# A pair of seven-product sets for the indexer's two column groups, and one operation for the low parts of a turned block

## The chip, the cores and the metric

The kernel runs on one core of a Trainium2 chip, as one launch. The metric is the device time of the launch in microseconds, the median of several runs. The core's engines work from queues of their own and wait for each other only where one needs what another made: TensorE (PE, with PEld for its weight loads), VectorE (DVE), ScalarE (ACT), GpSimd (POOL) and SyncE (SP), whose queue issues nearly all DMAs.

## The reference: what is computed

Two layers over 256 tokens of 2048 features, everything in float32. Each layer is a mixer and an MLP, each behind an RMS norm and added to the residual:

```
for i in range(DEPTH):                      # DEPTH = 2
    h = rms_norm(x, norm_mix[i])
    x = x + (stick_breaking_mixer if i % 2 == 0 else dsa_mixer)(h, ...)
    h = rms_norm(x, norm_mlp[i])
    x = x + square(relu(h @ w_up[i])) @ w_down[i]      # 2048 -> 8192 -> 2048
```

The change is in the second mixer, `dsa_mixer`:

```
q, k, v, qi, ki, wi = split(h @ w_in, [2048, 512, 512, 1024, 64, 16])
q = rms_norm(q, q_gain);  k = rms_norm(k, k_gain)      # per head of 128
score = sum over 16 heads of wi * relu(qi . ki)        # the indexer, heads of 64
sel   = the 64 best keys of each token, chunk-causal
p     = softmax(q . k[sel] + bias);  out = (p @ v[sel]) @ w_out
```

The indexer's queries `qi` are 1024 columns of that projection: two groups of 512.

## The kernel before, in words

**Splitting.** A float32 product is made of three products of rounded operands: activation and weight are each split into a high part and the rest. The activations lie transposed, as `xT` (features on the partitions, 16 tiles of 128, high and low part). A weight arrives block by block: an *item* is one block of 256 rows by 512 columns, held as 128 x 1024. SP loads it to `wraw` (L2006), ACT writes its high part `wh` (L2023), DVE the rest, `wl` (L2024). PE then does 12 matmuls of 512 columns (L628; L619 where an item is first in its section): 8 with `wh` against high and low activation, then 4 with `wl`. There are four buffers each for `wh` and `wl`, so the split of an item can start once the matmuls of the fourth one before it are through. A column group of 512 over the 2048 features is 8 items.

**Seven products.** In the MLPs, the output projection and the first mixer, two column groups of one matrix are mostly taken as a *pair*: of the 8 row blocks four go in two sets, `a` and `b`, and in each set a 2 x 2 block product is done with seven products (Winograd's form of Strassen's), not eight. A product has 6 matmuls; its weight is a sum of blocks (the rooms X, Y, Z: three DVE additions, L973, L976, L985, and one addition in an accumulating DMA on POOL's queue), its activation a sum S of blocks of `xT` (one whole addition and four quarter additions on DVE, L1079 and L1049 to L1052, then a split of the sum on ACT, L1060, and DVE, L1064). Half of the products are read back through seeds (copies of an accumulator, L1011 to L1028). The names `s1a` to `s7b` are the products of the two sets, `G0` to `G3` and `H0` to `H3` the items that stay plain.

**The second mixer.** `mixer_b` runs, before the change: 16 plain items for `qi` (two groups side by side), two short items for `ki` and `wi`, 8 items for `k`, then `q0 q1 q2 v q3` of 8 items each, and last the output projection, which is done in a pair already. Behind an item other work is hung (`post`): `k_done` (norm of k: two scalings L1783, 8 squares with sums on ACT L1789, small steps for the root, a product L1795, two transposes, a DMA round trip), `score_step` (L1739: 8 matmuls a call, then ACT and DVE), the choice of the 64 best, `logits_step` (L1851), `turn_step`, `o_step` (L1901 to L1903).

**Borders.** Where a section ends, its four column blocks c0 to c3 of the residual become the next section's `xT`: DVE adds the accumulators to the residual `xs` (L937, in the MLP L1335) and transposes in 32 x 32 blocks (L492); SP writes to DRAM in four DMAs (`tu<-jx`, L499) and reads back turned (`jx<-tu`, L504); ACT writes the high part with the gain in 4 operations (L524), DVE the low part in 8 (L529). ACT takes the squares for the norm (L908, L566).

**Order.** The program is unrolled. A planner (`Plan`) gives each piece of this work a slot behind an item, from costs and due times (`LAT`, `AHEAD`, `CALM`), and every engine then works its queue strictly in the order of that program. The main loop loads `far` items ahead and splits a few items ahead of PE. A scheduler may move PE's matmuls a little.

## Time and profile before

| | us |
|---|---|
| median of three runs (1988.82 to 1989.66) | 1989.25 |
| span of the profiled execution | 1986.8 |
| of it PE busy | 1980.4 |
| DVE busy | 1785.0 |
| ACT busy | 1301.7 |
| POOL busy | 91.7 |
| second mixer on PE, first matmul to the next section's first | 1028.39 to 1327.30 |

The span lies 2.45 us below the median of the runs. A row of the timeline has the start, the time until the last instruction of the row is done, the engine, the line, the operation, output and input, and how many instructions the row holds; behind it, in brackets, how long the engine stood idle before it, and what ended that. Engines are pipelined: the next operation can start some 0.1 us before the printed end of the one ahead. In the table of windows, the columns are busy time and instructions (x) of each engine, then the granted PE clock, the DMA share and the rate.

### The profile page before, as it was taken

To read this page: it belongs to the slowest core of one execution; us is meant where nothing else is said; L and a number is where in the kernel's file an instruction comes from. 1 tells how busy PE (TensorE), PEld (TensorE's weight loads), DVE (VectorE), ACT (ScalarE), POOL (GpSimd) and SP (SyncE) were. 2 spreads that over 40 slices of the span, in tenths; PEclk is the share of its full clock that TensorE was granted. 3 is DMA by queue.
4 is the path that set the end of the run, shared out by engine and by line. 5 is a ranking of instruction groups with operands and counts; after the bars stand their busy time and mean duration, and the time that the engine had idled before them with its cause. 6 is when DMAs were issued, how large, how long until landed. Compare 5 with 4: busy or idle time off the path is not lost.

```text
span 1986.8 us, 25525 instructions
## 1 busy us (share of the span) xinstructions
PE 1980.4 (100%) x8834; PEld 1635.3 (82%) x8834; DVE 1785.0 (90%) x1973; ACT 1301.7 (66%) x1573; POOL 91.7 (5%) x135
## 2 busy tenths in 40 slices
PE   9999999999999999999999999999999999999999
PEld 7888888888888888888888788788888888888887
DVE  6879869899999999989995898889998998998996
ACT  6567666667676676766764566666767676776664
POOL 0000100000000000020000000000000000000000
PEclk9999999999999999999999999999999999999999
DMA  9776766889788977889887698578887888788784
GB/s 350 215 238 189 218 211 181 275 289 292 244 259 257 278 235 239 288 277 295 247 291 235 190 264 255 153 264 281 290 265 244 254 269 271 224 286 276 256 244 146
DMA packets 233441, 498.44 MB, mean 251 GB/s; under 512 B 88608, under 2 KB 121440, under 8 KB 233312
## 3 DMA queue, kind: packets, MB, share of 16 engines
q1 hardware_dynamic: 216048, 455.81, 68.8%
q0 software_dynamic: 9216, 33.56, 9.4%
q10 hardware_dynamic: 8048, 7.45, 1.1%
q8 instruction: 69, 1.13, 0.2%
q14 instruction: 60, 0.49, 0.1%
HBM read 459.46 MB, written 37.22 MB: 250 GB/s over the span
## 4 chain that ended last, share of the span: by engine, by line
PE 99%; DVE 0%; DMA 0%; issue 0%; ACT 0%; SPq 0%; DVEq 0%
PE acc L1169 39%; PE acc L1151 26%; PE acc L628 17%; PE acc L732 5%; PE aux L1151 4%; PE aux L751 2%; PE acc L751 1%; PE acc L619 1%; PE aux L1851 0%; PE acc L1494 0%; PE aux L1554 0%; PE acc L1739 0%; PE aux L1169 0%; PE acc L1704 0%; PE aux L1556 0%; PE acc L1496 0%
## 5 line engine op out<-in xcount | busy, mean ns | idle before, releaser
L2024 DVE TENSOR_TENSOR wl<-wraw,wh 128x1024 fp32r<-128x1024 f32 (+1 forms) x670 | 805.5, 1217 | 134.6 <-ACT wh L2023 121.9
L2023 ACT ACTIVATE wh<-wraw 128x1024 fp32r<-128x1024 f32 (+1 forms) x670 | 700.0, 1053 | 317.8 <-PE acc L1169 110.7
L1169 PE MATMUL acc<-wh,xT 128*128 128x512 f32 x1152 | 284.6, 389 | 0.0
L1169 PEld LDWEIGHTS acc<-wh,xT 128*128 128x128 f32 x1152 | 216.2, 188 | 45.2 <-ACT wh L2023 0.3
L1169 PE MATMUL acc<-wh,half 128*128 128x512 f32 x1004 | 248.2, 389 | 0.0
L1169 PEld LDWEIGHTS acc<-wh,half 128*128 128x128 f32 x1004 | 188.5, 188 | 39.1
L1151 PE MATMUL acc<-wh,half 128*128 128x512 f32 x720 | 192.4, 389 | 0.0
L628 PE MATMUL acc<-wh,xT 128*128 128x512 f32 x736 | 185.5, 392 | 0.0
L628 PEld LDWEIGHTS acc<-wh,xT 128*128 128x128 f32 x736 | 137.6, 188 | 30.0 <-issue 1.7
L1151 PEld LDWEIGHTS acc<-wh,half 128*128 128x128 f32 x720 | 135.2, 188 | 28.1
L1169 PE MATMUL acc<-wl,xT 128*128 128x512 f32 x576 | 154.0, 389 | 0.0
L1169 PE MATMUL acc<-wl,half 128*128 128x512 f32 x502 | 134.4, 389 | 0.0
L1169 PEld LDWEIGHTS acc<-wl,xT 128*128 128x128 f32 x576 | 108.1, 188 | 22.5
L1151 PE MATMUL acc<-wl,half 128*128 128x512 f32 x360 | 110.8, 389 | 0.0
L1169 PEld LDWEIGHTS acc<-wl,half 128*128 128x128 f32 x502 | 94.2, 188 | 19.5
L628 PE MATMUL acc<-wl,xT 128*128 128x512 f32 x368 | 99.2, 391 | 0.0
L2023 ACT ACTIVATE wh<-Zb 128x1024 fp32r<-128x1024 f32 x60 | 63.5, 1058 | 41.5 <-PE acc L1169 14.4
L1151 PE MATMUL acc<-wh,xT 128*128 128x512 f32 x336 | 89.8, 389 | 0.0
L628 PEld LDWEIGHTS acc<-wl,xT 128*128 128x128 f32 x368 | 68.9, 188 | 15.0 <-DVE wl L2024 0.3
L732 PE MATMUL acc<-wh,xT 128*128 128x512 f32 x320 | 79.7, 391 | 0.0
L1151 PEld LDWEIGHTS acc<-wl,half 128*128 128x128 f32 x360 | 67.6, 188 | 14.0
L2024 DVE TENSOR_TENSOR wl<-Za,wh 128x1024 fp32r<-128x1024 f32 x60 | 73.4, 1223 | 0.7 <-ACT wh L2023 0.6
(404 smaller groups left out, 3087.2 us busy)
## 6 DMA issues: line engine op xcount, KB each, us to landing
wraw<-in_w_up_dram SPq DMA_DIRECT2D x228, 512.0 KB, 5.4
wraw<-in_w_down_dram SPq DMA_DIRECT2D x224, 512.0 KB, 5.1
wraw<-in_w_in_a_dram SPq DMA_DIRECT2D x88, 512.0 KB, 4.9
wraw<-in_w_in_b_dram SPq DMA_DIRECT2D x64, 512.0 KB, 4.8
jx<-tu SPq DMA_DIRECT2D x44, 512.0 KB, 5.8
tu<-y SPq DMA_DIRECT2D x128, 128.0 KB, 3.6
wraw<-in_w_out_a_dram SPq DMA_DIRECT2D x30, 512.0 KB, 3.6
wraw<-in_w_out_b_dram SPq DMA_DIRECT2D x30, 512.0 KB, 4.4
```

Of the source, the lines that this page charges most:

```text
L619: pin(pe.matmul(accs[key][t], L[:, j, part, t * P:(t + 1) * P], wx[:, j, :], start=(j == 0 and n == 0), stop=False))
L628: (keep if alone else pin)(pe.matmul(acc[t], L[:, KB * q + j, part, t * P:(t + 1) * P], wx[:, j, :], start=a and q == 0, stop=z and q == Q ...
L732: keep(pe.matmul(acc[:, t, :], L[:, KB * qs[i] + j, part, t * P:(t + 1) * P], wx[:, j, :], start=a and i == 0, stop=z and i == end - (last ...
L751: keep(pe.matmul(p, lhs(part, j), wx[:, j, :], start=to is None and a and n == sets[0], stop=to is None and z and n == sets[-1]))
L1151: keep(pe.matmul(o, lhs(part, j), wx[:, j, :], start=a and opens, stop=z, skip_group_check=True))
L1169: keep(pe.matmul(acc[:, t, :], L[:, KB * q + j, part, t * P:(t + 1) * P], wx[:, j, :], start=a and i == 0 and not self.sets, stop=z, skip_ ...
L2023: order(act.activation(wh[:, a], raw[:, a], AF.Copy))
L2024: order(dve.tensor_sub(wl[:, a], raw[:, a], wh[:, a].bitcast(F32)))
```

## The change

- `mixer_b` begins with `k` and `qi` together, in the order `ORDER_QI`. The two column groups of `qi` are a pair with two sets: 14 products of 6 matmuls and 8 plain items of 12 take the place of 16 plain items. The 8 items of `k` stand singly among the products, so `k` is complete, and `k_done` runs, behind `k7`, ahead of `s7a`; the short items for `ki` and `wi` follow the products.
- The sums' halves lie in `oT0`, and three of set a's and one of set b's rooms in `oT1`: the array for the attention's output is cut in two, and both are free until it is made. `nr`, `qTb`, `ph` and `pl` serve too. In this pair the additions for Y and the last one for Z (numbers 3 and 4) are accumulating DMAs.
- `turn_steps`: ACT scales the block in place in 4 operations and rounds it to the high part in a fifth, of 1024 elements; DVE makes the low part in one subtraction. This holds at all three inner borders (12 blocks).
- The planner also plans the loads and steps of `mixer_b` from its first item (`start = 0`, `strict`), and the numbers of the hung-on work move with the items (+6 for most).

```diff
-ADD = lambda p, s: True
+ADD = lambda p, s: (3,)
...
+ORDER_QI = ("k0 k1 k2 k3 s1a s1b k4 s5a k5 s5b k6 s6a s6b k7 s7a s7b s3a s3b s2a s4a s2b s4b i0 i1 "
+            "G0 G1 G2 G3 H0 H1 H2 H3")
+FIRST_USE = (0, 2, 5, 8)
...
     def turn_steps(c, col):
 
-        def views():
+        def part(i):
+            return xT[:, 4 * c:4 * c + 4, i, :].rearrange("p k (t a q) -> p t k a q", t=2, a=4)
+
+        def high(z):
             for j in range(4):
                 kt = 4 * c + j
-                h, l = (xT[:, kt, i, :].rearrange("p (t a q) -> p t a q", t=2, a=4)
-                        for i in range(2))
-                yield j, gains[:, col + kt:col + kt + 1], h, l
-
-        def high(z):
-            for j, g, h, l in views():
-                keep(act.activation(h, z[:, :, j], AF.Copy, scale=g))
+                keep(act.activation(z[:, :, j], z[:, :, j], AF.Copy,
+                                    scale=gains[:, col + kt:col + kt + 1]))
+            keep(act.activation(part(0), z, AF.Copy))
 
         def low(z):
-            for j, g, h, l in views():
-                for t in range(2):
-                    keep(dve.scalar_tensor_tensor(l[:, t], z[:, t, j], g, h[:, t].bitcast(F32),
-                                                  op0=OP.mult, op1=OP.subtract))
+            keep(dve.tensor_sub(part(1), z, part(0).bitcast(F32)))
...
-            h = self.plan.step("A", 1.6, lambda: high(by_token(z.tile)), after(z_in), uses=[z])
-            self.plan.step("V", 2.0, lambda: low(by_token(z.tile)), after(h), [("mm", n + min(4 * c, by))],
+            h = self.plan.step("A", 2.2, lambda: high(by_token(z.tile)), after(z_in), uses=[z])
+            self.plan.step("V", Plan.V, lambda: low(by_token(z.tile)), after(h), [("mm", n + by)],
                            uses=[z])
...
     def mixer_b():
         items = []
         weave = Weave(items)
+        weave.plan.start, weave.plan.strict = 0, True
...
-            st["oT"] = mk([P, HEADS, 2, S], "oT", F32R)
+            st["sums"] = mk([P, 2, 2, 4 * KB, P], "oT0", F32R)
+            st["rooms"] = mk([P, 4, KB, 512], "oT1")
...
-        for s, q in side_by_side(2, QB):
-            tokens_out(items, ("qi", s), w_in_b, 0, 3072 + 512 * s, lambda: xT, q,
-                       lambda acc, s=s: qi_done(s, acc))
-        items[10].post.append(stats)
-        items += [ki_part(0), ki_part(1)]
-        items[-1].post.append(ki_done)
-        k0 = len(items)
-        for q in range(QB):
-            tokens_out(items, "k", w_in_b, 0, 2048, lambda: xT, q, k_done)
+        def index_columns():
...
+            home.make["a"] = {name: lambda i=i: st["rooms"][:, i] for i, name in enumerate("XYZ")}
+            home.make["b"] = {"X": lambda: st["rooms"][:, 3], "Y": lambda: block_room(mk([P, 8, P], "ph")),
+                              "Z": lambda: block_room(mk([P, 8, P], "pl"))}
+            p = Pair(weave, w_in_b, 0, [3072, 3584], lambda: xT, lambda s, part: st["sums"][:, "ab".index(s), part],
+                     home=home)
+            for q in range(QB):
+                tokens_out(items, "k", w_in_b, 0, 2048, lambda: xT, q, k_done, alone=True)
...
+            for name in ORDER_QI.split():
+                items.append({"k": ks, "i": ki}[name[0]][int(name[1])] if name[0] in "ki" else p.by[name])
+            for i, s in enumerate("ab"):
+                weave.sums_from(lambda i=i: xT[:, 4 * i:4 * i + 4], [], [], [("mm", p.by["s5" + s])],
+                                lambda part, i=i: st["sums"][:, i, part], "sum",
+                                lambda i=i: mk([P, 8, P], ("nr", "qTb")[i]))
+            weave.adds = lambda p, s: (3,) if p.home is weave.home else (3, 4)
+            weave.sets_of(p, None)
+            weave.seeds(p, None)
...
-        for m, d in enumerate((6, 6, 8, 8, 10, 10, 12, 12)):
-            at(k0 + d, score_step, m)
+        for m, i in enumerate((34, 34, 36, 36, 38, 38, 40, 40)):
+            at(i, score_step, m)
...
-        weave.spread(weave.plan.run(weave.plan.start, {"jx": 3}))
+        for i in (3, 9):
+            weave.plan.busy[i] += [("A", 2.2), ("V", 1.2)]
+        weave.plan.busy[74] += [("PE", 0.9), ("A", 1.1)]
+        weave.spread(weave.plan.run(weave.plan.start, {"jx": 3, "sum": 2}))
```

Three places in the programs show what the new order does. DVE's queue at the start of the second mixer, before (L2024 is the split, L1335 and L492 the border's add and transposes, L529 the low part; the last row is the low part of the block c2):

```order
L1335 SCALAR_TENSOR_TENSOR xs<-acc,rs_3458,xs 128x512 x2
L1685 TENSOR_TENSOR gqk<-gains 128x1
L2024 TENSOR_TENSOR wl<-wraw,wh 128x1024
L492 STREAM_TRANSPOSE jx<-xs 128x4x128 x2
L582 TENSOR_REDUCE rs_m<-ss 128x2
L2024 TENSOR_TENSOR wl<-wraw,wh 128x1024
L583 TENSOR_SCALAR rs_m<-rs_m 128x2
L2024 TENSOR_TENSOR wl<-wraw,wh 128x1024 x2
L529 SCALAR_TENSOR_TENSOR xT<-jx,gains,xT 128x128 x8
```

and after the change (L2097 is the split, L1101 a sum's whole addition, L1071 to L1074 its quarters, L990 the room X):

```order
L2097 TENSOR_TENSOR wl<-wraw,wh 128x1024 x2
L1101 TENSOR_TENSOR nr<-xT 128x1024
L500 STREAM_TRANSPOSE jx<-xs 128x4x128 x2
L586 TENSOR_REDUCE rs_m<-ss 128x2
L1101 TENSOR_TENSOR qTb<-xT 128x1024
L1071 TENSOR_TENSOR nr<-nr 128x256
...
L1074 TENSOR_TENSOR qTb<-qTb 128x256
L2097 TENSOR_TENSOR wl<-wraw,wh 128x1024
L990 TENSOR_TENSOR oT_8665<-oT_8665,wraw 128x1024
L2097 TENSOR_TENSOR wl<-wraw,wh 128x1024
L990 TENSOR_TENSOR oT_8665<-ph,wraw 128x1024
L534 TENSOR_TENSOR xT<-jx,xT 128x2x4x128
```

Between the split of `k3` (the second of the first row) and that of `s1a` (the last but four) stand the two whole sums, the transposes of c3, eight quarter sums and the small steps of the norm; quarters and small steps are what the "..." leaves out.

ACT's queue from the split of `k4` on, after the change (L2096 the split, L529 and L531 the high part of the block c3, L1033 and L1037 seeds, L1828 the squares of `k_done`):

```order
L2096 ACTIVATE wh<-wraw 128x1024
L2096 ACTIVATE wh<-oT_8665 128x1024
L529 ACTIVATE jx<-jx,gains 128x2x4x32 x4
L531 ACTIVATE xT<-jx 128x2x4x128
L2096 ACTIVATE wh<-wraw 128x1024
L1033 ACTIVATE acc<-acc 128x512
...
L2096 ACTIVATE wh<-wraw 128x1024
L1828 ACTIVATE junk,nsq<-acc,rs 128x128 x8
L577 ACTIVATE rs_y<-nsq 128x8
L578 ACTIVATE rs_y<-rs_y 128x8
L2096 ACTIVATE wh<-wraw 128x1024 x2
```

The high part of c3 stands ahead of the split of `k5` (the row behind L531), and all 8 squares and the two steps of the root stand between the split of `s3a` (the row behind the "...") and those of `s3b` and `s2a` (the last row). Before, plain items of 12 matmuls and single splits lay among those squares.

ACT's queue at the border to the second MLP, before (L524 the high part, L908 and L566 squares):

```order
L2023 ACTIVATE wh<-wraw 128x1024 x5
L524 ACTIVATE xT<-jx,gains 128x256 x4
L908 ACTIVATE junk,ss<-xs 128x512 x2
L2023 ACTIVATE wh<-wraw 128x1024
L524 ACTIVATE xT<-jx,gains 128x256 x4
L2023 ACTIVATE wh<-wraw 128x1024 x2
L566 ACTIVATE junk,ss<-xs 128x512
L524 ACTIVATE xT<-jx,gains 128x256 x4
```

and after:

```order
L2096 ACTIVATE wh<-wraw 128x1024 x2
L529 ACTIVATE jx<-jx,gains 128x2x4x32 x4
L531 ACTIVATE xT<-jx 128x2x4x128
L2096 ACTIVATE wh<-wraw 128x1024 x2
L529 ACTIVATE jx<-jx,gains 128x2x4x32 x4
L531 ACTIVATE xT<-jx 128x2x4x128
L919 ACTIVATE junk,ss<-xs 128x512 x2
L2096 ACTIVATE wh<-wraw 128x1024
L529 ACTIVATE jx<-jx,gains 128x2x4x32 x4
L531 ACTIVATE xT<-jx 128x2x4x128
L2096 ACTIVATE wh<-wraw 128x1024 x4
```

Before, the high part of c2 (the last row) is the third of its kind and has the splits of the MLP's items 0, 1 and 2 ahead of it; after, the one of c2 (the last L529 and L531) has only the split of item 0 ahead, and the splits of items 1, 2 and 3 stand in the row behind it.

## The prediction

> **What bounds the kernel now.** I read the page first: the span, the busy times, the chain of work that ended last, and the two rows of the weight splits.

> ```profile
> span 1986.8 us, 25525 instructions
> PE 1980.4 (100%) x8834; PEld 1635.3 (82%) x8834; DVE 1785.0 (90%) x1973; ACT 1301.7 (66%) x1573; POOL 91.7 (5%) x135
> PE 99%; DVE 0%; DMA 0%; issue 0%; ACT 0%; SPq 0%; DVEq 0%
> L2024 DVE TENSOR_TENSOR wl<-wraw,wh 128x1024 fp32r<-128x1024 f32 (+1 forms) x670 | 805.5, 1217 | 134.6 <-ACT wh L2023 121.9
> L2023 ACT ACTIVATE wh<-wraw 128x1024 fp32r<-128x1024 f32 (+1 forms) x670 | 700.0, 1053 | 317.8 <-PE acc L1169 110.7
> ```

> PE is the path: all but 6.4 us of the span, 99% of the chain. Fewer matmuls pay in full where PE stays fed, and every gap costs in full. DVE, at 90%, is what may leave PE unfed; each split costs ACT 1.05 and DVE 1.22 us whether its item has 12 matmuls or 6. Next, the windows in which the change works:

> ```profile
> 1030.00:1040.00 10.00, 10.00 (x46) 8.29 (x45) 7.59 (x16) 6.74 (x14) 0.00 (x0) 1.00 0.93 305
> 1040.00:1050.00 10.00, 10.00 (x46) 8.29 (x45) 6.96 (x16) 5.33 (x8) 0.00 (x0) 1.00 0.76 258
> ...
> 1220.00:1270.00 50.00, 48.70 (x229) 38.98 (x228) 41.39 (x61) 31.83 (x73) 0.86 (x1) 1.00 0.59 196
> ```

> In the first two PE has no gap, and DVE is free for 2.4 and 3.0 us of 10. The third already loses 1.3 us.

> **The change part by part.** The timeline of PE shows the section's start and one item:

> ```profile
> 1028.39 1.07 PE L619 MATMUL acc<-wh,xT 128*128 128x512 f32 x4
> ...
> 1039.27 1.98 PE L628 MATMUL acc<-wh,xT 128*128 128x512 f32 x8
> 1041.09 1.07 PE L628 MATMUL acc<-wl,xT 128*128 128x512 f32 x4
> 1041.99 1.98 PE L628 MATMUL acc<-wh,xT 128*128 128x512 f32 x8
> ```

> An item of 12 takes 2.72 us (1039.27 to 1041.99), a matmul 0.2267. *Gain:* 16 x 12 = 192 matmuls become 14 x 6 + 8 x 12 = 180: **-2.72 us**. The score steps are gathered in pairs three times, not once. A pair and a single step:

> ```profile
> 1097.12 1.58 PE L1739 MATMUL acc<-kiT,w 64*128 64x128 f32 x16
> ...
> 1104.97 0.93 PE L1739 MATMUL acc<-kiT,w 64*128 64x128 f32 x8
> ```

> 2 x 0.93 - 1.58 = 0.28 per pair: **-0.6** for two more.

> *DVE at the start.* In the order of the change, the split of `s1a` stands behind work of which most was not there. Its prices, with the block c2's low part of before:

> ```profile
> 1028.59 1.41 DVE L1335 SCALAR_TENSOR_TENSOR xs<-acc,rs,xs 128x512 f32<-128x512 f32 x2 [0.35 <-PE acc L1169]
> ...
> 1029.98 1.22 DVE L2024 TENSOR_TENSOR wl<-wraw,wh 128x1024 fp32r<-128x1024 f32 x1
> 1031.12 1.30 DVE L492 STREAM_TRANSPOSE jx<-xs 128x512 f32<-128x512 f32 x2
> ...
> 1038.45 2.19 DVE L529 SCALAR_TENSOR_TENSOR xT<-jx,gains,xT 128x128 fp32r<-128x128 f32 x8
> ```

> ```profile
> L1049 DVE TENSOR_TENSOR jx<-jx 128x256 f32<-128x256 f32 x24 | 10.1, 422 | 0.0
> ```

> Printed times include some 0.08 us that overlaps the next operation (1029.98 to 1031.12 is 1.14). From 1028.59: add c3 1.33, low part of c1 as one operation 1.14, two splits 2.28 and `gqk` 0.06, two whole sums 2.28, transposes 1.22, eight quarters at 0.33 = 2.64, six small steps of the norm at 0.2 = 1.2, split of `s1a` 1.22. That is 13.4: 1042.0. PE starts `s1a` behind four items of `k`, at 1039.27, and wants its `wl` four matmuls later, at 1040.18: **1.9** of stall. X (1.14) and the split of `s1b` end at 1044.3, wanted at 1043.4: **0.9**. The other X and the low part of c2 end at 1046.6; `k4` would start at 1044.75: **1.85**. The shorter low parts (2.19 to 1.22) are in these numbers; without them each wait is 1 us longer.

> *c3.* ACT's split of `k5` now waits behind the high part of c3. The reads of c2 and c3 before, on SP and ACT:

> ```profile
> 1028.28 0.34 SPq L504 DMA_DIRECT2D jx<-tu  x1
> ...
> 1038.31 0.33 SPq L504 DMA_DIRECT2D jx<-tu  x1
> ```

> ```profile
> 1034.54 1.69 ACT L524 ACTIVATE xT<-jx,gains 128x256 fp32r<-128x256 f32 x4
> ...
> 1044.97 1.69 ACT L524 ACTIVATE xT<-jx,gains 128x256 fp32r<-128x256 f32 x4
> ```

> Issue to use is 6.3 and 6.7 us. The read of c3 stands on SP behind a weight load that needs the buffer read by set a's X: 1043.3, so c3 is there at 1049.6. The high part is 1.69 + 1.06 for the added rounding, less 0.1 of overlap: 2.65, and the split 1.06: 1053.3. `k5` could start at 1050.7: **2.6** (1.5 if the read lands a microsecond earlier, 4.5 if two later). On DVE its split, c3's low part, the split of `s5b` and the low part of sum b (four at 1.14 to 1.22) end at 1057.9; `s5b` is due at 1056.0: **1.9**.

> *k_done* now comes where items have 6 matmuls (1.36 us) and ACT does 8 squares in a row. Its rows before:

> ```profile
> 1102.42 1.41 DVE L1783 TENSOR_SCALAR nr<-acc,rs 128x512 f32<-128x512 f32 x2
> ...
> 1112.58 0.16 DVE L575 TENSOR_TENSOR rs_z<-rs_y 128x8 f32<-128x8 f32 x1
> ...
> 1113.39 1.22 DVE L1795 TENSOR_TENSOR nr<-nr,nry 128x1024 f32<-128x1024 f32 x1
> ```

> ```profile
> 1104.46 0.35 ACT L1789 ACTIVATE junk<-acc,rs 128x128 bf16<-128x128 f32 x1
> ...
> 1104.93 0.37 ACT L1789 ACTIVATE junk<-acc,rs 128x128 bf16<-128x128 f32 x1
> ```

> A square with the reading of its sum takes 0.47 (1104.46 to 1104.93), eight 3.8. `k7` ends at 1067.5 (1057.9 plus `s5b`, `k6`, `s6a`, `s6b`, `k7` = 9.5); scalings 1.4, squares 3.8, three small steps 0.6 and a split of 1.06 give 1074.4 for `s3b`, which could start at 1071.5, after three products: **2.9**. On DVE the four small steps 0.8 (1112.58 to 1113.39), the product, transposes and split (3.5) stand before its `wl`: 1077.8 against 1075.3: **2.5**. Before, items of 2.72 us and their splits lay among the squares and nothing waited. Index section: 1.9 + 0.9 + 1.85 + 2.6 + 1.9 + 2.9 + 2.5 = **14.55**.

> *Border to the second MLP.* c2 is the third block; its chain, and the start of that MLP:

> ```profile
> 1327.30 1.98 PE L1169 MATMUL acc<-wh,xT 128*128 128x512 f32 x8
> ```

> ```profile
> 1316.62 1.29 DVE L937 TENSOR_TENSOR xs<-acc,xs 128x512 f32<-128x512 f32 x2 [1.31 <-PE acc L1169]
> 1317.83 1.30 DVE L492 STREAM_TRANSPOSE jx<-xs 128x512 f32<-128x512 f32 x2
> ```

> ```profile
> 1324.28 1.71 ACT L524 ACTIVATE xT<-jx,gains 128x256 fp32r<-128x256 f32 x4 [1.46 <-DMA jx<-tu]
> ...
> 1330.66 1.70 ACT L524 ACTIVATE xT<-jx,gains 128x256 fp32r<-128x256 f32 x4
> ```

> ACT reached c2 3.36 us after the MLP's start, and had split items 0 to 2 by then. Now item 1's split stands behind it: 3.36 + 2.65 + 1.06 = 7.0, wanted at 2.72: **4.3**. DVE's split of item 1 waits for that, and behind it stand the add and transposes of c3, c2's low part and item 2's split (five at 1.2, to 12.9, wanted at 11.5): **1.4**. Bounds of the two: 3.4 if c2 had landed a microsecond before its use, 9 if it takes 3.2 us more than here.

> *Logits.* In the order of the change, the third group of logits and the nine products of `o_step` follow each other, where 7 plain matmuls lay among them before, and DVE has two scalings of the next `nr` ahead of the third bias addition, which frees the bank for the last six.

> ```profile
> 1223.49 0.69 DVE L1853 SCALAR_TENSOR_TENSOR w<-aux,bias 128x512 f32<-128x512 f32 x1 [0.33 <-PE aux L1851]
> ```

> ```profile
> 1225.60 0.40 PE L1901 MATMUL aux<-ph,vh 128*128 128x512 f32 x1
> ```

> Before, the addition was done at 1224.1, 1.5 us ahead of those six. Now it comes 1.4 later and they 1.6 earlier (7 x 0.2267): 1.5 of stall, none if DVE runs ahead there, 3.9 with two splits (1.2 each) in front; I take **2**. The low parts at the first mixer's border are off the path: 0.

> Sum: -2.72 - 0.6 + 14.55 + 5.7 + 2 = **+18.9**. The profiled span of 1986.8 becomes 2005.7; the median of the runs stands 2.45 above the span: **2008 us**.

> **The rivals.**
> 1. *Fed in time* (not slower). The one mechanism is a DVE that runs ahead: if the splits of `k2` and `k3` are through before the section begins (2.3 us), the queue of 13.4 us ends 0.2 us before `s1a` wants its `wl`, X, the low parts and the later splits move up with it, and what c2, c3 and `k_done` cost must lie inside that lead. 1989.25 - 3.3 = 1985.9. For it: DVE is free for 5.4 of the 20 us from 1030. Against it: at 1029.98 and 1031.12 DVE still goes from one operation to the next, and ACT's two late blocks don't depend on DVE's lead. It decides from 2 us of lead at the section's start.
> 2. *Only a part.* The reads of c2 and c3 land early and the small steps slip in between; the 5.4 us of k_done stay, and the 4.65 at the start: -3.3 + 10 = +6.7, 1996. For it: c2's use at 1330.66 has no wait printed, so it may have been there some time.
> 3. *Heavier.* c2 and c3 as late as the bounds above (3.3 and 1.9 more) and logits at 3.9: 2008 + 7.1 = 2015. For it: at 1324.28 ACT stood 1.46 us idle for c1's read.
> 4. *A clock that falls after a wait.* The opening matmuls:

> ```profile
> 1.12 3.78 PE L413 MATMUL acc<-ones 128*128 128x512 f32 x8 [1.12 <-DVE ones L385]
> ```

> These are some 0.45 us apart, twice the 0.2267 of later, for about 4 us: a PE that had stood idle was slow. If the 4.3 us at the border bring that back, the next 4 us hold 9 matmuls in place of 18, 2 us more; if `k5`'s or `s3b`'s wait does too, 4: 2010 to 2012. [...]

> **How the numbers follow.** Forecast 0.60, heavier 0.13, clock 0.08, only a part 0.11, fed in time 0.08. The measurement tells 0.2% (4 us) from no change: 1985.3 to 1993.2. Forecast, heavier, clock and most of the partial case are slower: 0.88; fed in time gives 0.03 faster and 0.05 same, the partial case's lower end 0.03 same, and I add 0.01 to faster for a gain that I don't see. The forecast's own range, from the lower bounds (c3 -1.1, border -2.3, logits -2) and the upper (+1.9, +3.3, +1.9), is 2002.6 to 2015. To hold 8 in 10 it takes in half of the partial case and the clock's cases: **1995 to 2017**.

> **What would show it.** In the changed profile: PE idle of 1 to 2 us before rows of `s1a`, `s1b`, `k4` ended by DVE's `wl` or `xT`; of 2 to 4 before `k5` and `s3b` ended by ACT's `wh`; some 4 us within 3 us of the second MLP's start; the mixer some 15 us longer while PE's busy time falls by about 3. It is wrong if PE shows no gap over 0.5 us in the first 45 us of the mixer, or if the second MLP starts without one.

## The result, and the profile after

The changed kernel takes 2012.66 us (median of 4 runs, 2010.5 to 2019.43) against 1989.03 for the kernel before: a ratio of 1.0124, with an interval of 1.0112 to 1.0137. It is slower by 23.6 us. The profiled execution is the slowest of the four, 2019.43 us with a span of 2017.6. Two further sets of runs of the same kernel gave medians of 2015.29 and 2011.71, with profiled spans of 2012.9 and 2010.4; the last is nearest to the usual time, so numbers below are given for it too. One of all the runs below, of the kernel with the old turn put back, took 2711.62 us at a granted clock of 0.688 and is left out.

The page of the changed kernel: span, busy times, chain.

```profile
span 2017.6 us, 25476 instructions
PE 1989.8 (99%) x8822; PEld 1639.7 (81%) x8822; DVE 1793.0 (89%) x1913; ACT 1323.2 (66%) x1596; POOL 95.2 (5%) x139
PE 94%; DVE 2%; DMA 2%; ACT 1%; issue 1%; SPq 0%; DVEq 0%; ACTq 0%
```

PE has the 12 matmuls less (8822 for 8834) and yet 9 us more busy time; its share of the chain falls from 99% to 94%. PE's waits by releaser (us in total, times, longest); before, the longest after the first microseconds was 0.7.

```profile
PE aux L1941 <- DVE w L1892: 4.3, 1, 4.3
PE acc L1192 <- ACT wh L2096: 3.8, 3, 3.3
PE acc L1174 <- DVE wl L2097: 3.4, 3, 1.5
PE acc L1174 <- ACT wh L2096: 3.3, 1, 3.3
PE aux L1174 <- DVE oT L1946: 3.1, 1, 3.1
PE acc L632 <- ACT wh L2096: 2.6, 2, 2.4
PE acc L632 <- DVE xT L534: 1.3, 1, 1.3
```

From the top: the third bias addition of the logits; item 1 of the second MLP; the `wl` of `s1a`, `s1b`, `s3b`; the `wh` of `s3b`; a sum of the output pair; `k5`; `k4`. Most of the same waits in PE's timeline (start, duration, what; in brackets the idle time before and who ended it):

```profile
1043.33 0.74 PE L1174 MATMUL acc<-wl,xT 128*128 128x512 f32 x2 [1.28 <-DVE wl L2097]
...
1054.61 3.01 PE L632 MATMUL acc<-wh,xT 128*128 128x512 f32 x8 [2.36 <-ACT wh L2096]
...
1076.32 2.07 PE L1174 MATMUL acc<-wh,oT 128*128 128x512 f32 x4 [3.27 <-ACT wh L2096]
1079.89 1.22 PE L1174 MATMUL acc<-wl,oT 128*128 128x512 f32 x2 [1.50 <-DVE wl L2097]
...
1358.26 2.86 PE L1192 MATMUL acc<-wh,xT 128*128 128x512 f32 x8 [3.31 <-ACT wh L2096]
```

Two things are to be seen. Each of these waits (`s1a`, `k4`, `k5`, `s3b` twice, the MLP's item 1) has the place and the releaser that the prediction gave. And behind the longer ones the matmuls themselves are slow: the 4 at 1076.32 take 2.07 us, where 4 took 1.07 before.

To add up I take the start of each 128x512 matmul to the start of the next and count what is over 0.2267 us: 0.2 more is a slow matmul, any other excess a wait. (A wait so counted is some 0.15 longer than the idle time in brackets, which ends with the modelled end of the matmul before.)

| | before | after, span 2017.6 | after, span 2010.4 |
|---|---|---|---|
| waits | 2.5 | 26.6 | 24.2 |
| slow matmuls | 1.5 | 9.3 | 5.3 |
| 12 matmuls less | 0 | -2.7 | -2.7 |
| sum against before | | +29.2 (span: +30.8) | +22.8 (span: +23.6) |

So of 23.6 us some 22 are waits, some 4 a slower PE behind them, and the matmuls saved give 2.7 back. What no row accounts for is 1.6 us in the first trace and 0.8 in the other.

### The profile page after: what moved, and what is told of

It is laid out like the page before. It is cut to its first block, busy times and chain, and to the rows that moved or that the text cites. A ratio compares the mean times of both kernels' runs of the same rounds, so it can differ in the third digit from the quotient of the medians.

```text
span 2017.6 us, 25476 instructions
## 1 busy us (share of the span) xinstructions
PE 1989.8 (99%) x8822; PEld 1639.7 (81%) x8822; DVE 1793.0 (89%) x1913; ACT 1323.2 (66%) x1596; POOL 95.2 (5%) x139
## 4 chain that ended last, share of the span: by engine, by line
PE 94%; DVE 2%; DMA 2%; ACT 1%; issue 1%; SPq 0%; DVEq 0%; ACTq 0%
PE acc L1192 38%; PE acc L1174 26%; PE acc L632 14%; PE acc L736 5%; PE aux L1174 4%; PE aux L755 2%; PE acc L755 1%; DMA jx<-tu 1%; DVE wl L2097 1%; PE aux L1890 0%; DMA tu<-jx 0%; ACT wh L2096 0%; PE acc L1517 0%; PE aux L1577 0%; DMA qTb<-in_w_out_b_dram 0%
## 5 line engine op out<-in xcount | busy, mean ns | idle before, releaser
L2097 DVE TENSOR_TENSOR wl<-wraw,wh 128x1024 fp32r<-128x1024 f32 (+2 forms) x668 | 800.7, 1214 | 137.4 <-ACT wh L2096 134.9
L2096 ACT ACTIVATE wh<-wraw 128x1024 fp32r<-128x1024 f32 (+2 forms) x668 | 696.9, 1053 | 297.3 <-PE acc L1192 113.4
L1192 PEld LDWEIGHTS acc<-wh,xT 128*128 128x128 f32 x1216 | 228.3, 188 | 53.3 <-ACT wh L2096 5.9
L1192 PE MATMUL acc<-wl,xT 128*128 128x512 f32 x608 | 163.6, 391 | 0.0
L632 PEld LDWEIGHTS acc<-wh,xT 128*128 128x128 f32 x616 | 115.4, 189 | 30.5 <-ACT wh L2096 3.4
L1192 PEld LDWEIGHTS acc<-wl,xT 128*128 128x128 f32 x608 | 114.6, 189 | 24.7 <-DVE wl L2097 0.9
L2096 ACT ACTIVATE wh<-Zb 128x1024 fp32r<-128x1024 f32 x60 | 63.5, 1059 | 40.5 <-PE acc L1192 16.3
L632 PE MATMUL acc<-wl,xT 128*128 128x512 f32 x308 | 83.7, 394 | 0.0
L1174 PEld LDWEIGHTS acc<-wh,xT 128*128 128x128 f32 x360 | 68.2, 189 | 14.3
L2097 DVE TENSOR_TENSOR wl<-Za,wh 128x1024 fp32r<-128x1024 f32 x60 | 73.1, 1218 | 0.4 <-ACT wh L2096 0.4
```

The source lines that it names most:

```text
L632: (keep if alone else pin)(pe.matmul(acc[t], L[:, KB * q + j, part, t * P:(t + 1) * P], wx[:, j, :], start=a and q == 0, stop=z and q == Q ...
L1174: keep(pe.matmul(o, lhs(part, j), wx[:, j, :], start=a and opens, stop=z, skip_group_check=True))
L1192: keep(pe.matmul(acc[:, t, :], L[:, KB * q + j, part, t * P:(t + 1) * P], wx[:, j, :], start=a and i == 0 and not self.sets, stop=z, skip_ ...
L2096: order(act.activation(wh[:, a], raw[:, a], AF.Copy))
L2097: order(dve.tensor_sub(wl[:, a], raw[:, a], wh[:, a].bitcast(F32)))
```

## The experiments

**The same kernel again**, beside the experiments of the first and the third group, to see which waits are fixed.

> The changed kernel as it is, for a second trace of it. If its time is made of fixed waits and of a clock that falls behind the long ones (the theory), PE's waits stand at the same places with the same lengths within 0.3 us (k5 2.4, s3b 3.3 and 1.5, logits 4.3, the output pair's sum 3.1, second MLP 3.3), while the stretches of matmuls 0.427 us apart lie differently, and the times spread between 2009 and 2020 us. If the spread comes from the waits themselves (late transfers), their lengths differ by several microseconds.

> The changed kernel as it is, beside the three that follow, on their chip. 2010 to 2016 us, as in the two comparisons ahead of it (2012.7 and 2015.3).

Measured: 2015.29 us, ratio 1.0129 (1.0115 to 1.0143), and 2011.71, 1.0114 (1.0099 to 1.0129). The waits, counted as above, in the three traces (spans 2017.6, 2012.9, 2010.4):

| wait | predicted | measured |
|---|---|---|
| `s1a`, `s1b`, `k4` | 1.9, 0.9, 1.85 | 1.44, 0.76 to 0.78, 1.46 to 1.48 |
| `k5`, then `s5b` | 2.6, 1.9 | 2.53 and 0; 1.93 and 1.59; 1.66 and 1.58 |
| `s3b`: `wh`, `wl` | 2.9, 2.5 | 3.44, 1.89 to 2.54 |
| logits | 2 | 4.51; 3.40; 2.79 |
| sum of the output pair | none | 3.30; 2.91; 3.00 |
| MLP: item 1, item 2's `wl` | 4.3, 1.4 | 3.47 and 0; 2.77 and 1.22; 1.91 and 1.25 |

The first row and `s3b`'s `wh`, which engine queues alone set, repeat to 0.02 us, within the 0.3 that was expected. `k5`, the logits and the MLP's item 1, where a DMA comes in, differ by 0.9 to 1.7, which was not expected; and of what the first of two takes, the second is in part spared.

**The squares of `k_done` spread out.** One square per item on a copy that DVE has scaled, the rest and the turn nine items on:

```
-  def normed(acc):
+  def normed(acc, spread=None):
...
+      for i in range(8):
+          later(1 + i, square, i // GRP, i % GRP)
+      later(9, rest)
+      later(9, spread, r)
```

> The changed kernel with the 8 squares of k_done taken one behind each of the next 8 products, from the scaled copy, and the root after them. The theory (ACT's and DVE's queues of k_done stand before the splits of s3b): the waits of 3.3 and 1.5 us at s3b go, with up to 2 us of slow matmuls behind them: 5 to 7 us less than the changed kernel, 2005 to 2008. The rival (ACT and DVE have too little room among products of 1.36 us, so the wait only moves): less than 2 us gained, 2010 or more, with new waits before s2a to s4b.

2005.37 us, 1.0084 (1.007 to 1.0098), 9.9 less than the unchanged copy of the same group. ACT's queue there, first of the change, then of this kernel:

```profile
1068.51 1.05 ACT L2096 ACTIVATE wh<-wraw 128x1024 fp32r<-128x1024 f32 x1
1070.75 0.37 ACT L1828 ACTIVATE junk<-acc,rs 128x128 bf16<-128x128 f32 x1 [1.19 <-DVE nr L1822]
...
1075.23 1.99 ACT L2096 ACTIVATE wh<-wraw 128x1024 fp32r<-128x1024 f32 x2
```

```profile
1068.84 2.00 ACT L2114 ACTIVATE wh<-wraw 128x1024 fp32r<-128x1024 f32 x2
1070.73 0.30 ACT L1829 ACTIVATE junk<-nr 128x128 bf16<-128x128 f32 x1
...
1071.02 1.05 ACT L2114 ACTIVATE wh<-wraw 128x1024 fp32r<-128x1024 f32 x1
```

In the change nothing is split between 1069.6 and 1075.2: 1.2 us for the scalings on DVE, eight squares 3.9, three small steps. In this kernel a split follows every square, both waits of `s3b` are gone (3.44 and 2.54 in the copy), and no new one stands up to `s4b`. So the term `k_done` is shown. The other 4 us between the two traces are slow stretches: none stands in this one (granted clock 1.000). That holds for this trace alone: the kernel's other four runs, at granted clocks of 0.997, took 2003.56 to 2008.27 us.

**The read of c3 ahead of a weight load**, one place up in SP's queue:

```
  weave.spread(...)
+ for i, k in {3: 1}.items():
+     weave.plan.loads[i] -= k
```

> The changed kernel with one weight load on SP's queue moved behind the read of the block c3. The theory (that load waits for the buffer which set a's X reads, and holds the read up): the read is issued some 5 us earlier, the wait of 2.4 us before k5 goes, with up to 1.4 us of slow matmuls behind it; s5b may then wait for sum b's low part, up to 2: between 2009 and 2012, 1 to 4 us less. The rival (c3 is late since its transposes and writes are late, not for its place in the queue): no change, 2011 to 2014.

2010.87 us, 1.0111 (1.0097 to 1.0125), 4.4 less than the copy. SP and ACT of the change, then of this kernel:

```profile
1044.47 0.35 SPq L2079 DMA_DIRECT2D wraw<-in_w_in_b_dram  x1
1045.01 0.34 SPq L512 DMA_DIRECT2D jx<-tu  x1
...
1050.82 1.71 ACT L529 ACTIVATE jx<-jx,gains 128x256 f32<-128x256 f32 x4 [5.25 <-DMA jx<-tu]
```

```profile
1043.69 0.34 SPq L512 DMA_DIRECT2D jx<-tu  x1
1044.14 4.21 SPq L2081 DMA_DIRECT2D wraw<-in_w_in_b_dram  x3
...
1047.57 1.70 ACT L529 ACTIVATE jx<-jx,gains 128x256 f32<-128x256 f32 x4 [3.03 <-DMA jx<-tu]
```

Counted from `s1a`'s first `wl`, which is 1.02 us earlier in this trace (1042.31 and 1043.33), the read is issued only 0.3 us earlier, not some 5, but used 2.2 us earlier: from issue to use 3.9 us in place of 5.8 (5.3 and 4.8 in the other two traces of the change). What the weight load ahead of it costs is in landing, not in the issue. Why the issue hardly moves is told by what SP waits for from 1030 to 1050 (in total, times, longest), in the change and here:

```profile
SPq L2079 <- DVE oT L990: 6.1, 2, 4.7
```

```profile
SPq L512 <- DMA tu<-jx: 4.8, 1, 4.8
```

In the change the load ahead of the read waits for set a's X, as predicted. With the load out of the way, SP stands as long for the landing of the read's own four writes `tu<-jx`.

`k5` has no wait in this trace and `s5b` has 0.39. But `k4`'s matmuls run at half rate just ahead (8 in a window of 3.42 us at a granted clock of 0.50), and some 1.5 us lost there hide part of what `k5` would wait for. So I take the time from the mixer's first matmul to the first of `k6`, which lies behind all five waits of the start (`s1a`, `s1b`, `k4`, `k5`, `s5b`): 28.2 us here, 28.5 and 28.6 in two kernels below that move the read too, 30.4, 29.9 and 29.6 in the three traces of the change. Moving the read is worth 1 to 2 us there.

**The second MLP's first splits ahead of c2**: the order's end for that section moves as far as it does for planned sections with a deep start.

```
- end = max(end, i + DEEP + 1 if plans[sec].deep else 0)
+ end = max(end, i + DEEP + 1 if plans[sec].deep or plans[sec].strict else 0)
```

> The changed kernel in which the main loop again splits three items ahead across the border to the second MLP, as before the change. The theory (the high part of c2 stands ahead of the split of the MLP's item 1): the wait of 3.3 us behind item 0 goes, with up to 1.4 us of slow matmuls, and single waits under 1.5 us come in its place: 2 to 4 us less, 2009 to 2011. The rival (c2's transfer is late for the MLP anyway): the wait stays, within 1 us of 2012.7.

2009.9 us, 1.0107 (1.0093 to 1.0121), 5.4 less than the copy. ACT at the border, the change first:

```profile
1346.54 1.04 ACT L2096 ACTIVATE wh<-wraw 128x1024 fp32r<-128x1024 f32 x1
1354.46 1.71 ACT L529 ACTIVATE jx<-jx,gains 128x256 f32<-128x256 f32 x4 [6.88 <-DMA jx<-tu]
...
1357.16 3.88 ACT L2096 ACTIVATE wh<-wraw 128x1024 fp32r<-128x1024 f32 x4
```

```profile
1343.61 1.99 ACT L2096 ACTIVATE wh<-wraw 128x1024 fp32r<-128x1024 f32 x2
1349.15 1.71 ACT L529 ACTIVATE jx<-jx,gains 128x256 f32<-128x256 f32 x4 [3.55 <-DMA jx<-tu]
```

In the change ACT stands idle for 6.88 us in front of c2's read with a split behind it that needs nothing from c2. With two splits ahead, item 1 starts without a wait; 0.64 is left before the `wl` of a later item and 1.17 some 15 us on.

A caution on the times: the copy that these three kernels are compared with was the slowest of the three. Against all twelve runs of the unchanged kernel (2009.7 to 2019.43 us, median 2012.3) the three gains are 6.9, 1.4 and 2.4 us. The last two lie inside that spread, so what is shown of c3 and of the border rests on their waits and not on their times.

**All three together.**

> The changed kernel with the squares of k_done spread, the read of c3 moved ahead of the weight load, and the splits across the border three ahead, together. If the waits are separate, the three gains add: 9.9 + 4.4 + 5.4 less than the changed kernel's 2015.3 in the same comparison, 1995 to 1998; what is left over before's time is the start of the section (3.7), logits and the output pair's sum (6 to 7), less the 3.3 saved. If they share a cause (DVE's total work) the gain is under 14 us, 2001 or more.

2004.21 us, 1.0075 (1.0061 to 1.0089): a miss, some 6 to 9 us above what was expected. The bound of the rival (2001 or more) is met, but the waits don't say that the three share a cause: they fall by 12.0 us, from 26.7 to 14.7, and singly by 6.0, 4.4 and 3.5. The times had been compared with the slow copy: against the twelve runs the single gains add up to 10.7 us, and this kernel's is 8.1. The trace of the spread squares, besides, had no slow stretch, and this one loses some 4 us to them. What is left of waits: the start 3.7, `s5b` 0.7, the logits, the output pair 3.3, the border 1.7. So the gains in time can't be added up, and those in waits nearly can.

**The low part as one operation, alone and undone.** Into the kernel before, the new way of turning a block (4 scalings in place, one rounding on ACT, one subtraction on DVE); into the change, the old one (4 operations on ACT, 8 on DVE).

```
  def low(z):
-     for j, g, h, l in views():
-         for t in range(2):
-             keep(dve.scalar_tensor_tensor(l[:, t], z[:, t, j], g, h[:, t].bitcast(F32),
...
+     keep(dve.tensor_sub(part(1), z, part(0).bitcast(F32)))
```

> The kernel before with the new turn_steps alone (high part in 4 + 1 operations, low part in one). The theory (the pair's place in the queues makes the change slow, the turned blocks little): within 2 us of before, 1988 to 1991; DVE is relieved by 1 us per block, ACT loaded with 1 us more. The rival (the longer high part makes the borders late by itself): 4 us and more, 1993 or above, with waits behind the start of each section.

> The changed kernel with the turn_steps of before. By the prediction's sum DVE's low parts of c1 and c2 (2.19 instead of 1.22 us) add about 1 us to each of the waits before s1a and k4, and ACT's shorter high part takes about 1 us from those before k5 and at the second MLP: no net change beyond 2 us, 2011 to 2016. If the new turn_steps carry the loss: 2005 or less.

Alone: 1988.93 us, 1.0002 (0.9993 to 1.0011), no difference. The busy times of this kernel:

```profile
PE 1980.7 (100%) x8834; PEld 1634.9 (82%) x8834; DVE 1774.9 (89%) x1889; ACT 1314.8 (66%) x1585; POOL 91.7 (5%) x135
```

DVE is relieved of 10 us and ACT loaded with 13; the kernel before waited for neither.

Undone: 2013.04 us (three runs), 1.0122 (1.0106 to 1.0138), as the change. `s1a`'s wait grows to 2.40 (from 1.44) and `s1b`'s to 2.63 (from 0.78), as DVE has more to do, but `k4` falls to 0.36, `k5` to nothing: with `s5b` the five make 7.2 us, and in the three traces of the change 6.2, 7.2 and 6.9. Something later than DVE's queue sets their sum.

**DVE's queue at the start without the eight quarter additions.** The kernel leaves them out, so what it computes is not the reference's.

```
+ if z.ring == "sum":
+     return
```

> The changed kernel without the eight quarter additions of the index pair's two sums (2.64 us of DVE; the sums, and what is computed from them, are then not the reference's). The theory of the prediction (DVE's queue of 13.4 us sets the start of s1a, s1b and k4): the three waits there, 3.7 us together, fall to about 1; k5's wait stays near 2, since c3's read waits for set a's X, which is earlier by as much: 2 to 3 us less than the changed kernel. The rival (c3's read and ACT set the time at which k5 starts, whatever DVE does ahead): k5's wait grows by what the first three lose, no change within 1 us.

2017.66 us, 1.0149 (1.0132 to 1.0166): slower, with less work, which neither the theory nor the rival had expected. PE, ACT and SP at the place:

```profile
1055.77 3.78 PE L632 MATMUL acc<-wh,xT 128*128 128x512 f32 x8 [6.94 <-ACT wh L2098]
```

```profile
1051.98 1.70 ACT L529 ACTIVATE jx<-jx,gains 128x256 f32<-128x256 f32 x4 [10.97 <-DMA jx<-tu]
...
1043.61 0.34 SPq L512 DMA_DIRECT2D jx<-tu  x1
```

The waits of `s1a` and `s1b` are gone and `k4`'s is 0.58: that part of DVE's queue was rightly priced (2.6 us taken away, 3.1 of wait gone). More than that comes back: 1.0 before a small step of the norm and 7.1 before `k5`, since ACT stands for c3's read, which takes 8.4 us from issue to use here (4.8 to 5.8 in the change). The read is issued no earlier than in the change, 14.7 us after the mixer's first matmul (14.9 there), although the weight load ahead of it goes out 3.4 us earlier: again SP stands for the four writes, 3.2 us. Why the read then takes longer is open. Two weight loads follow it on SP within 1 us here, where in the change the first follows after 1.7; that these two slow it down is likely, and no run tests it. So the waits of the first 30 us lie in series, and the last of them, c3, sets the end: moving c3's read brings the first matmul of `k6` forward, from some 30 us after the mixer's first to some 28.5, and shortening DVE's queue puts it off to 33.1.

**The clock measured by itself.** In the kernel before, copies on POOL of a low part onto itself (2 to 7, at 12 items of the first MLP) make PE wait for a chosen time in a stage that is fed.

```
+ for _ in range(PROBE.get(i, 0)):
+     w = parts[i][1]
+     pool.tensor_copy(w, w.bitcast(F32))
```

> The kernel before with 12 waits put on PE in the first MLP, 22 items apart: 2 to 7 copies of wl onto itself on POOL ahead of one item's low-part matmuls, twice over. The theory of the clock: behind a wait of some 3 us or more the matmuls of 512 columns come 0.427 us apart for a few microseconds, behind a wait under 2 us none do; a length between is slow at one site and not at another. The rival (slow matmuls come from what the engines do around these waits, not from the wait): matmuls keep 0.2267 us behind waits of every length.

2051.11 us. Matmuls of 0.427 us instead of 0.2267 behind each wait that the trace has (the two places with two copies show none):

| wait, us | 0.77 | 1.83 | 2.39 | 3.35 | 4.42 | 5.47 | 6.54 | 6.71 | 6.77 | 7.30 |
|---|---|---|---|---|---|---|---|---|---|---|
| slow matmuls | 0 | 0 | 0 | 7 | 11 | 10 | 12 | 7 | 13 | 13 |
| lost on them, us | 0 | 0 | 0 | 1.5 | 2.4 | 2.1 | 2.6 | 1.6 | 2.8 | 2.7 |

PE's rows at two of them, waits of 1.83 and 6.77:

```profile
716.18 1.21 PE L1170 MATMUL acc<-wl,half 128*128 128x512 f32 x4 [1.67 <-POOL wl L2074]
...
629.97 2.08 PE L1170 MATMUL acc<-wl,xT 128*128 128x512 f32 x4 [6.61 <-POOL wl L2074]
631.84 3.61 PE L1170 MATMUL acc<-wh,xT 128*128 128x512 f32 x8
```

**Dummy matmuls in two of the longest waits**: 14 ahead of `s3b`, 12 ahead of the MLP's item 1, into a bank that nobody reads.

```
...
+ for _ in range(n):
+     keep(pe.matmul(warm_to, ones, ones.unsqueeze(1).to_broadcast([P, 4, P]), start=True, stop=True))
```

> The changed kernel with 14 matmuls of a constant, whose result nobody reads, ahead of s3b and 12 ahead of the second MLP's item 1, so that PE works through most of those two waits; what it waits for stays as late as it is. If a clock that falls behind a wait costs part of the time: no matmul comes 0.427 us apart behind these two places, which saves up to 2.3 + 1.5 us at s3b and 1.7 at the border: 2 to 5 us less than the changed kernel in the same comparison, with the other waits as they were. If the slow matmuls have another cause: no gain, or a loss where the filling outlasts the wait.

2012.53 us, 1.0121 (1.0106 to 1.0136), and 2011.71 for the copy beside it: a miss, nothing is gained.

```profile
1070.40 3.33 PE L2151 MATMUL aux<-ones 128*128 128x512 f32 x14
1073.84 1.20 PE L1174 MATMUL acc<-wh,oT 128*128 128x512 f32 x4
1077.41 0.73 PE L1174 MATMUL acc<-wl,oT 128*128 128x512 f32 x2 [2.37 <-DVE wl L2097]
```

The 4 behind the fill do run at full rate (1.20 us, for 2.07 in the change), but the `wl` that follows comes when DVE has it, so what they gain is waited for (2.54 in place of 1.89), and that wait leaves its own slow matmuls (two groups of 4 take 1.56 and 1.83 us, for 1.07 at full rate). In the change the slow 4 lay inside a time that was lost anyway. At the border 12 matmuls last 2.72, longer than the 1.91 of the copy's wait, though the 1.25 before item 2's `wl` goes in return.

**The logits' second and third group one and two items later**, on top of all three:

```
- ((logits_step, (51, 58, 66, 77)), ...
+ ((logits_step, (51, 59, 68, 77)), ...
```

> The kernel of the three repairs together (squares spread, c3's read ahead, border) with the second and third logits_step hung one and two items later, so that the third lies behind the first o_step. If the wait at the logits (2.3 to 4.3 us, and 1 behind it) comes from the third bias addition standing late in DVE's queue while o_step needs its bank: the wait falls under 2, up to 2.8 us of slow matmuls with it, 2 to 4 us under the 2004.2 of the three repairs, 2000 to 2002. If the logits are late since the whole chain of the indexer's choice is: the wait comes back in another place, 2004 or more.

2004.62 us, 1.0084 (1.0069 to 1.0099), no better than 2004.21, as the rival had it. The logits' wait is gone, and this stands 14 us behind its old place:

```profile
1248.21 1.94 PE L1883 MATMUL aux<-ident,nr 128*128 128x128 f32 x8 [4.32 <-DVE nr L1840]
```

By my reading, which no run tests, DVE's work of that stretch is the same, and whichever of its results PE wants first is waited for.

## Why the prediction was right, and where it was not

- *The gain* is 12 matmuls, 2.7 us, as counted. The score steps do come in three pairs of 1.58 us, for one pair before: by the same prices the 0.6 of the prediction. It is not in the table above and would add to what no row accounts for.
- *DVE at the start* is right in kind and high by a fifth (3.7 us for 4.65). The split of `s1a` was to end at 1042.0, 13.6 us after the mixer's first matmul. Here the mixer starts at 1030.11, and the split

```profile
1042.06 1.22 DVE L2097 TENSOR_TENSOR wl<-wraw,wh 128x1024 fp32r<-128x1024 f32 x1
```

ends at 1043.3, 13.2 after: 0.4 too much in a queue of 13.4. "Each wait is 1 us longer" without the short low parts holds for `s1a` (0.96) and not for the rest: they lie in series with c3, which the sum had as a further term and not as the one that sets the end of them all. So the five can't be summed one by one.
- *c3* (2.6) measured 1.7 to 2.5, with the predicted time of issue for a reason that is only half of it. The sum has the read go out 14.9 us after the mixer's first matmul, when set a's X frees a buffer for the load ahead; it goes out at 14.9 to 15.0 in the three traces of the change. But its own four writes land only then, at 14.2 to 14.9, so that with the load out of the way it still goes out at 14.5 to 14.9. That the two times are nearly one was luck. What the load ahead does cost is 1 to 2 us of the landing, by the run that moved it.
- *k_done* (2.9 and 2.5) measured 3.44 and 1.9 to 2.5, and is shown by the run that spread the squares.
- *The border* was too high (5.7 in all; 3.2 to 4.0). The step that failed is "ACT reached c2 3.36 us after the MLP's start": here it did so 2.4, 1.7 and 0.8 us after in the three traces (in the first at 1354.46, with the MLP started at 1352.07). The order on ACT as the cause is shown by the run that moved the splits ahead.
- *Logits* were too low. From 1230 to 1270 PE stood idle for 1.3 us in the kernel before, and from 1230 to 1290 for 4.9, 3.8 and 4.0 in the three traces of the change: 2.5 to 3.6 net, for 2. DVE's addition and what stands ahead of it, with ACT and SP:

```profile
1239.89 1.22 DVE L2097 TENSOR_TENSOR wl<-wraw,wh 128x1024 fp32r<-128x1024 f32 x1 [0.74 <-ACT wh L2096]
...
1243.64 0.67 DVE L1892 SCALAR_TENSOR_TENSOR w<-aux,bias 128x512 f32<-128x512 f32 x1
```

```profile
1238.80 1.06 ACT L2096 ACTIVATE wh<-wraw 128x1024 fp32r<-128x1024 f32 x1 [6.13 <-DMA wraw<-in_w_out_b_dram]
```

```profile
1225.81 8.19 SPq L469 DMA_DIRECT2D td<-jx  x8
1234.09 11.70 SPq L2079 DMA_DIRECT2D wraw<-in_w_out_b_dram  x8
```

The upper bound ("with two splits in front") had the mechanism: a split stands in front, and it is late because its weight load waits on SP behind 8 writes `td<-jx` that take 8.2 us to issue. I had not followed SP there. That the load is the first cause is read from the trace; no run moved it.
- *Missing from the sum:* a sum of the output pair, 2.9 to 3.3 us. Two low parts of `o_step`, which free a bank for it, now stand behind three splits and a low part of another sum on DVE:

```profile
1297.21 2.35 DVE L2097 TENSOR_TENSOR wl<-wraw,wh 128x1024 fp32r<-128x1024 f32 x2
...
1300.62 1.28 DVE L1946 TENSOR_TENSOR oT<-aux,oT 128x512 fp32r<-128x512 f32 x2
```

This section is not in the diff; its order moved with the numbers of the items, and I compared the queues only where the diff is.
- *The clock* was a rival at 0.08 and should have been a term of the forecast, since it does not exclude the waits but follows from them: +3.8 us in the trace near the median, +7.8 in the slowest. Its price there, 9 matmuls for 18 in some 4 us, was close (10 matmuls in a window of 3.41 us at 0.50, 16 in the next, at 1.00).

Two of the signs that the prediction named came out otherwise: the mixer is 20 to 23 us longer, not 15, and PE's busy time rises by 3 to 9 us where it was to fall by 3, as matmuls at half rate count as busy (PE is busy for all 3.41 us of that window).

So 2008 came out for 2012.66 because the waits were right in sum (22.25 predicted; 21.7 and 24.1 net of before) and the clock was left out. That the sum was right is partly luck: the index section came to 11.6 to 13.2 us for 14.55 and the border to 3.2 to 4.0 for 5.7, and the output pair, which no term had, took the place of what they lack. No variant beat the kernel before: the best, 2004.21, still has 14.7 us of waits against 2.7 saved.

## What to carry to other kernels

A form that saves matmuls but leaves each item's splits as they were makes the items shorter than their supply: here 2.7 us were bought for 24, and what had to be right was the order of the queues of DVE, ACT and SP around every item that got shorter, in sections too whose text did not change. Waits behind one another are not terms to be taken away singly: find the one that sets the last (here a DMA read that can go out only when its own writes have landed, and lands later behind a weight load, 5.8 us from issue to use for 3.9), since shortening an earlier one can move time into it, or add to it (2.6 us taken off DVE's queue put the first matmul of `k6` off from some 30 us after the mixer's first to 33.1). Price a wait of more than 2 us with the clock that it may cost behind it (here 3.8 us in one trace and 7.8 in another; a wait of 2.53 us was followed by half rate, one of 2.77 was not), and take a gain of a few us between single runs for a gain only if the waits in the trace fell too.

## What the runs showed of the hardware

```profile
1052.17:1055.58 3.41, 1.05 (x5) 0.82 (x5) 1.58 (x3) 3.38 (x5) 0.00 (x0) 1.00 1.04 273
1055.58:1058.99 3.41, 3.41 (x10) 2.63 (x9) 3.41 (x4) 2.33 (x3) 0.00 (x0) 0.50 0.90 316
1058.99:1062.41 3.42, 3.42 (x16) 2.63 (x16) 3.42 (x4) 1.94 (x2) 0.00 (x0) 1.00 0.00 1
```

```profile
1043.48:1046.89 3.41, 1.50 (x7) 0.60 (x5) 3.41 (x5) 1.05 (x1) 1.42 (x2) 1.00 0.64 160
1046.89:1050.31 3.42, 3.42 (x8) 2.74 (x9) 3.42 (x5) 2.71 (x6) 0.30 (x1) 0.50 1.02 266
```

In the trace of 2017.6, cut so throughout, each window at 1.00 in which PE worked for 0.12 to 1.11 us is followed by one at 0.50, and each in which it worked for 1.79 or more by another at 1.00; a fed window at half rate loses, by estimate, 1.7 us (half of 3.41). In the second fence no single wait is over 1.5 us: two of them, 0.76 and 1.47, lie in one window. Where the same waits were cut otherwise by the grid, no half rate followed, as in the change at that place, where the grid cuts the 0.76 (it ends at 1045.60) and 1.85 us of work are left in the window of the 1.48:

```profile
1045.34:1048.75 3.41, 1.85 (x7) 1.24 (x8) 3.41 (x5) 0.22 (x1) 1.47 (x2) 1.00 0.94 244
```

In the windows at 1.00 so cut in six traces, 1.50 us of PE and less were followed by half rate, 1.84 and more were not, and from 1.66 to 1.79 it went both ways: 1.79 was followed by it in the kernel of all three together; 1.66, 1.73, 1.75 and, in the change, 1.79 were not. A window that was itself at 0.50 was followed by another with 0.77, 2.07 and 2.37 us of PE in it, and by 1.00 with 2.93 and more. From this I estimate that a wait under some 1.6 us (3.41 less 1.79) costs no clock by itself here. Waits of 2 to 4 us went both ways: 2.53 (`k5` in the change), which left 1.05 us of work in one window, and 2.54 (the `wl` of `s3b` behind the fill) were followed by half rate; 2.77 (the MLP's item 1), which the grid cut so that 2.49 and 1.73 were left in two, 2.39 (in the kernel with the copies) and, with the squares spread, 3.24 were not. That fits the runs of the change lying 10 us apart, with 7 such windows in the trace of 2017.6, at a granted clock of 0.994, and by estimate 3 or 4 in that of 2010.4, at 0.997. Of the twelve runs, the four with a granted clock of 0.994 or 0.995 took 2013.85 to 2019.43 us, the others, at 0.996 to 0.998, 2009.7 to 2014.7. That the grid is the whole cause of the spread is not shown, since waits on DMAs differ too.
